# A mixture of experts with soft routing on one core: routing weights read back from DRAM, and weight blocks fetched one by one

## The chip, the core and the metric

The kernel runs on one core of a Trainium2 chip. A core has TensorE for matrix products (PE in the profile; its weight loads stand apart as PEld), VectorE (DVE) and ScalarE (ACT) for elementwise work, GpSimd (POOL), which here mostly issues DMAs, and SyncE (SP), which only issues DMAs. TensorE writes its results to PSUM[...]; everything else on the chip lies in SBUF. The metric is device time in microseconds (us), the median of several runs. A change of under 2% either way counts as "the same".

## The reference

Every one of 8192 rows has 512 values and 8 router logits. The softmax of the logits gives 8 routing weights, and the output row is the sum over the 8 experts of the weight times the row's product with that expert's 512 x 2048 matrix.

```python
batch, seq, hidden, n_experts, expert_hidden = 16, 512, 512, 8, 2048
probs = np.exp(router_logits - logits_max)
probs = probs / np.sum(probs, axis=-1, keepdims=True)
for e in range(n_experts):
    expert_out = np.matmul(x, expert_weights[e])
    output += probs[:, :, e:e+1] * expert_out
```

## The kernel before

The sum over experts is written as one large product: the rows, each scaled by its eight weights and laid side by side, times the stacked expert matrices. That product is cut into 2 x 2 blocks, and a scheme of the Strassen-Winograd kind (seven products of sums and differences in place of eight) is applied to it, in part on two levels. `B11` ... `B22` are the four blocks of the stacked matrices (in the code `11`, `12`, `21`, `22`); each comes as four tiles `w` of 1 MB in float16 (128 x 8 x 512). `z` are the scaled rows, made on VectorE from `xT` (a block of 256 rows, transposed) and `pT` (the routing weights of these rows, the same on all partitions).

The program has a start (rows 0 to 511 at once, without the scheme), four sub-products (numbers 1, 5, 2 and 4), and a main phase, which does the remaining products for all rows. TensorE, VectorE and the other engines each run their instructions in a fixed order; SyncE and GpSimd each issue their DMAs in a fixed order, and an issue that has to wait holds up those behind it.

Two kinds of routing weights are made in the start. A small softmax takes the logits of 512 rows only; a large one takes all rows, and its result goes to DRAM (`p_dram`), from where `load_p` fetches it for a block of 256 rows, the same row to all partitions:

```python
def softmax_of_all():
    pf = softmax(lg_all, J)
    ...
    for r in range(R):                      # four stores
        sp(p_dram[:, :, ds(r * J, J)], ph[ds(r * NHQ, NHQ)])

def load_p(h, first):
    pT = xpool.tile([P, HE, HQ], f16, name="pT", tag="x")
    sp(pT, p_dram[h, ds(first, HE), :].partition_broadcast(P))
    return pT
```

`sp` issues a DMA from SyncE, `pool` one from GpSimd. For rows 512 to 1023 (two blocks of 256) the kernel before does not use `load_p`. It makes diagonal matrices from the small softmax and multiplies a matrix of ones with them, so that TensorE itself spreads the weights over the partitions:

```python
def early_xp1(j, d):
    t, rows = j // 2 - 2, ds(j % 2 * P, P)
    ps = bank()
    for c in range(C):                      # transposes x with an identity
        mm(ps[:, ds(c * P, P)], xs0[:, j, ds(c * P, P)], ident, c == 0, c == C - 1)
    evacuate(xp1[t][0][:, :, rows], ps.rearrange("p (c t) -> p c t", c=C), 0)
    ps = bank()                             # spreads the routing weights
    mm(ps, ones, d.rearrange("p e t -> p (e t)"), True, True)
    evacuate(xp1[t][1][:, :, rows], ps.rearrange("p (e t) -> p e t", e=HE), 1)
```

`evacuate` copies a bank to SBUF, on VectorE for an even last argument and on ScalarE for an odd one. The call stands in the start, among the products for rows 0 to 511:

```python
for n in range(2):
    ps = [bank() for _ in range(4)]
    for e in range(HE):
        ...                                 # 16 matmuls for each n and e
        if n == 1:
            for j in ((4, 5), (6, 7), (), ())[e]:
                early_xp1(j, ds_[j - 4])
            if e == 1:
                sums[0]()
    for j in range(4):
        o = half()
        act(nc.scalar.copy(o, ps[j]))
        sp(kept[1][j // 2][n]..., o)        # results kept in DRAM, 256 KB each
    if n == 0:
        ph0.append(early_p(1))              # the small softmax
        softmax_of_all()
        ds_ = [diag_j(j) for j in range(4, 8)]
        w, sums = inner_sums(b11, new_w())
```

Sub-product 1 follows, with the two blocks as its `xp`. It makes four `z` from them, three sums and a difference of these, and the matching sums `w` of the weight tiles; seven products `prod(p)` of eight matmuls each follow, twice (for `u` = 0 and 1), in the order 1, 2, 5, 6, 3, 7, 4:

```python
a11, a12 = (mul(*xp[0], e0, 2, 0, HQ) for e0 in (0, 2))
a21, a22 = (mul(*xp[1], e0, 2, 0, HQ) for e0 in (0, 2))
s1 = new(a21, a22, ADD)
s2 = new(s1, a11, SUB)
s4 = new(a12, s2, SUB)
tt(a21, a11, a21, SUB)
z = {1: a11, 2: a12, 3: s4, 4: a22, 5: s1, 6: s2, 7: a21}
```

The main phase needs twelve weight tiles at once (`w6`, `w7`, `w3`) out of fifteen that the pool has. `load` has a gate: a tiny memset of the new tile on VectorE, so that the DMA is not issued before VectorE has come to that place. The four tiles of B22 (`w3`) are loaded at the end of sub-product 4, without the gate. In the first pass of the main phase (`q == 0`) they are first used after eight groups of 16 matmuls (four with `w6`, four with `w7`):

```python
def weights_of_main():
    ...
    w3.update({kn: load(22, kn, False) for kn in BLOCKS})
...
for j, tn in enumerate(QUARTERS):           # four groups with w6
    if j > 1:
        rows.load_kept(j)
    x = bank()
    act(nc.scalar.copy(x, rows.m1[tn]))
    ...
    plain(x, 6, w6, tn, False)
    v = half("u")
    tt(v, x, rows.m5[tn], ADD)
```

Of the kernel before, what the change touches and what calls it, by code (L numbers as in the profile page):

```python
# [32 lines left out]
def kernel(  # L33
# [7 lines left out]
    nc = tc.nc  # L41
# [90 lines left out]
    def sp(o, i):  # L132
        note(nc.sync.dma_start(out=o, in_=i))  # L133
# [84 lines left out]
    def cast_x(j):  # L218
        pool(xs0[:, ds(j, 2), :], x_f[ds(j * HQ, HQ), :].rearrange(ROWS[j // 4], p=P))

    def load_lg0(t):
        rows = lg_f.rearrange("(q h) e -> q h e", h=2 * HQ)[ds(2 * t, 2), 0:HQ]
        tile_ = lg0[t].rearrange("p (q j) e -> p q j e", j=2)
        if t == 0:
            sp(tile_, rows.rearrange("q (p j) e -> p q j e", p=P))
        else:
            for q in range(2):
                sp(tile_[:, q], rows[q].rearrange("(j p) e -> p j e", p=P))
    lg0 = [cpool.tile([P, 4, E], f32, name=f"lg0_{t}") for t in range(2)]
    load_lg0(0)  # L230
    cast_x(0)
    cast_x(2)
    ident = cpool.tile([P, P], f16, name="ident")
# [10 lines left out]
    for e in range(2):  # L244
        cast_w(11, BLOCKS[3], e, b11[BLOCKS[3]])

    def early_p(t):
        return softmax(lg0[t], 4, cpool.tile([P, HE, 4], f16, name=f"ph0_{t}"))

    def diag(p):  # L250

        d = h_tile([P, 4, P], f16)
        tt(d, ident.unsqueeze(1).to_broadcast([P, 4, P]), p.to_broadcast([P, 4, P]), MUL)
        return d
# [6 lines left out]


    z0 = [zpool.tile([P, HE, C, P], f16, name="z", tag="z") for j in range(4)]
    ph0 = [early_p(0)]

    def diag_e(e):
        return diag(ph0[0][:, e].unsqueeze(2))

    def early_z0(e, d):
        for j in range(4):  # L270
# [3 lines left out]
            evacuate(z0[j][:, e], ps.rearrange("p (c t) -> p c t", c=C), j)  # L274


    ones = cpool.tile([P, P], f16, name="ones")
    nc.vector.memset(ones, 1.0)
    xp1 = [[xpool.tile([P, C, HQ], f16, name=name, tag="x") for name in ("xT", "pT")] for t in range(2)]

    def diag_j(j):
        return diag(ph0[1][:, :, ds(j % 4, 1)])

    def early_xp1(j, d):
        t, rows = j // 2 - 2, ds(j % 2 * P, P)
        ps = bank()
        for c in range(C):
            mm(ps[:, ds(c * P, P)], xs0[:, j, ds(c * P, P)], ident, c == 0, c == C - 1)
        evacuate(xp1[t][0][:, :, rows], ps.rearrange("p (c t) -> p c t", c=C), 0)
        ps = bank()  # L290
        mm(ps, ones, d.rearrange("p e t -> p (e t)"), True, True)
        evacuate(xp1[t][1][:, :, rows], ps.rearrange("p (e t) -> p e t", e=HE), 1)


    R = 4
# [4 lines left out]

    def load_logits():
        dve(nc.vector.memset(lg_all[:, 0, 0:1], 0.0))
        dve(nc.vector.memset(lg0[1][:, 0, 0:1], 0.0))
        load_lg0(1)
        for r in range(R):
            sp(lg_all[ds(r * NHQ, NHQ)], lg_v[r])

# [134 lines left out]
# [3 lines that stand above are left out]
            if n == 0 and e < 2:  # L445
                early_z0(e + 2, ds_[e + 2])
                if e == 0:
                    ds_.append(diag_e(3))
            for c in range(C):
                for j in range(4):  # L450
                    mm(ps[j], z0[j][:, e, c], b11[e // 2, n][:, e % 2 * C + c, :],
                       e + c == 0, e == HE - 1 and c == C - 1)
            if n == 1:
                for j in ((4, 5), (6, 7), (), ())[e]:
                    early_xp1(j, ds_[j - 4])
                if e == 1:
                    sums[0]()
        for j in range(4):
            o = half()
            act(nc.scalar.copy(o, ps[j]))  # L460
            sp(kept[1][j // 2][n].rearrange("(p j) m -> j p m", j=2)[j % 2], o)
        if n == 0:
            ph0.append(early_p(1))
            softmax_of_all()
            ds_ = [diag_j(j) for j in range(4, 8)]
            w, sums = inner_sums(b11, new_w())

    def weights_of_t1():
# [6 lines left out]
        yield  # L475
        ready[5] = yield from inner_weights(b)
    pinned[0] = False
    x_new.extend((4 + 2 * t, xp1[t][0]) for t in range(2))
    share(xs=3, r=4, o=8)
    sub_product(1, 0, P1, w, weights_of_t1(), 1,  # L480
                xp1, (sums[1], sums[3], sums[2]))
# [36 lines left out]
    def weights_of_main():  # L518
        for kn in BLOCKS:
            t, w7[kn] = load(22, kn), load(12, kn)  # L520
            yield
            tt(w7[kn], t, w7[kn], SUB)
        for kn in BLOCKS:
            w6[kn] = load("t2", kn)
        yield
        w3.update({kn: load(22, kn, False) for kn in BLOCKS})
    share(r=4, o=11)
    sub_product(4, 1, P2, ready[4], weights_of_main())

# [73 lines left out]
        rows.c11(j)  # L603
    pinned[0] = True
    o10 = None
    sums = inner_weights(w3)
    for q in range(NI):
        following = Rows(q + 1) if q + 1 < NI else None

        def ahead(make, k, following=following):  # L610
            if following:
                getattr(following, make)(k)

        def plain(ps, r, w, tn, start):
            t, n = tn
            for k in range(2 * K8):
                mm(ps, rows.z[r][k // K8][:, k % K8, ds(t * P, P)], w[k // K8, n][:, k % K8, :],
                   start, k == 2 * K8 - 1)


        xs, vs = [], []
        for j, tn in enumerate(QUARTERS):
            if j > 1:
                rows.load_kept(j)
            x = bank()
            act(nc.scalar.copy(x, rows.m1[tn]))  # L626
            if o10 and j == 0:
                o10()
            if j > 1 or q == 1:
                rows.c11(j)  # L630
            if j < 2:
                rows.s4(j)
            else:
                ahead("a11", j - 2)
# [3 lines that stand above are left out]
            xs.append(x)  # L638
            vs.append(v)

        banks = {}

        def seeded(b, v, scale=1.0):
            banks[b] = bank()
            act(nc.scalar.mul(banks[b], v, scale))  # L645
        if q:
            seeded("b", vs[0])
            seeded("d", vs[3], -1.0)
            if q == NI - 1:
                seeded("e", vs[3], -1.0)  # L650
        else:
            seeded(0, vs[0])
            seeded(1, vs[1])


        if q == 1:
            inner3 = finish(sums)
        if q:
            z3 = rows.inner()
        for j, tn in enumerate(QUARTERS):  # L660
            x, m5 = xs[j], rows.m5[tn]
            plain(x, 7, w7, tn, False)
            c21 = half("m")
            act(nc.scalar.copy(c21, x))  # L664
            rows.put(1, 0, tn, c21, accum_op=ADD)
            tt(m5, x, m5, ADD)
            rows.put(1, 1, tn, m5)
            if j < 2:
                ahead("s2", j)


        def early(j):
            if following:
                following.load_kept(j)
                if q:
                    following.c11(j)

        ahead("s3", 0)
        if q == 0:
            def c12(j, tn, rows=rows, vs=vs, banks=banks):  # L680
                act(nc.scalar.copy(vs[j], banks[j]))
                rows.put(0, 1, tn, vs[j])

            for j, tn in enumerate(QUARTERS):
                plain(banks[j], 3, w3, tn, False)
                if j < 2:
                    seeded(j + 2, vs[j + 2])
                if j < 3:
                    c12(j, tn)
                if j < 2:  # L690
                    early(j)
                    next(sums)
            ahead("s3", 1)
            o10 = lambda: c12(3, QUARTERS[3])
            rows = following
            continue

        def prod(p, b):
            if b not in banks:
                banks[b] = bank()  # L700
            for k in range(K8):
                mm(banks[b], z3[p][:, k, :], inner3[p][:, k, :],
                   p in (1, 5) and k == 0, k == K8 - 1)
            return banks[b]

        def put(j, *args, rows=rows, vs=vs):
            tt(vs[j], *args)
            rows.put(0, 1, QUARTERS[j], vs[j])

        v00, v01, v11, v10 = vs  # L710
        x = prod(1, "x")
        r1 = half("r")
        act(nc.scalar.copy(r1, x))  # L713
        put(0, prod(2, "b"), r1, ADD)
        early(0)
        r5 = prod(5, "q")
        tt(v11, r5, v11, ADD)
        prod(6, "x")
        tt(v01, x, v01, ADD)
        early(1)  # L720
        put(1, prod(3, "q"), v01, ADD)
        prod(7, "x")
        r3 = half("r")
        act(nc.scalar.copy(r3, x))  # L724
        put(2, x, v11, ADD)
        ahead("s3", 1)
        if q < NI - 1:
            d = prod(4, "d")

            def o10(put=put, r3=r3, d=d):  # L730
                put(3, r3, d, SUB)
        rows = following
# [35 lines left out]
```

## Time and profile before

| What | Before |
|---|---|
| median of 3 runs | 1434.25 us (1433.23 to 1434.26) |
| span of the profiled run | 1434.2 us |
| ScalarE busy | 271.0 us |
| GpSimd busy | 219.6 us |
| moved by DMA | 318.92 MB, 222 GB/s on average |
| longest stretch of TensorE in the chain of waits | 715.03 us, from 48.49 |

In the chain of waits a line is a stretch of the path that ended last: start, length, and what it was. In a timeline a line is a run of like instructions: start, length, engine, line of the kernel, operation, what it writes and reads, how many, and in brackets the idle time before it with what ended it. In the DMA view a line gives a queue or a kind of issue, its number, its size and the median time from issue to landing. A line of the waits names who waited for whom, the total, how often, and the longest.

### The profile page before, as it was taken

Reading aid. Unit: us, or ns where it says so; the run is one execution under the profiler, and the core shown is the slowest. Engines: PE = TensorE matmul, PEld = TensorE weight load, DVE = VectorE, ACT = ScalarE, POOL = GpSimd, SP = SyncE. Lnnn points to the kernel's source line nnn. Section 1 sums busy time; section 2 is a strip of 40 time slices with the busy share of each in tenths; the row PEclk is TensorE's granted clock in tenths of the full one; section 3 lists DMA queues with packets and bytes.
Section 4 is the critical chain, followed back from the end, with each engine's and each line's share of the span. In section 5 each row is a group of like instructions: output and inputs, shape, how many; then the busy total and the mean of one; then the engine's idle time right before and its main releaser. Section 6 shows DMA issues by size and latency. Waiting matters only on the chain.

```text
span 1434.2 us, 18172 instructions
## 1 busy us (share of the span) xinstructions
PE 1424.9 (99%) x6654; PEld 647.9 (45%) x6654; DVE 1032.0 (72%) x1173; ACT 271.0 (19%) x472; POOL 219.6 (15%) x344
## 2 busy tenths in 40 slices
PE   9999999999999999999999999999999999999998
PEld 4444444444444444444444444444444444444444
DVE  6967585656686867766767687777777877877773
ACT  3211111111111111111111211111111111111111
POOL 3111000110001000001000222222222222222220
PEclk9999999999999999999999999999999999999999
DMA  9899967899649994467766967777777767778764
GB/s 196 185 249 266 274 160 191 183 258 259 208 148 301 352 338 147 132 191 222 213 248 206 298 188 238 237 237 233 229 220 226 210 212 214 231 234 242 220 199 103
DMA packets 192041, 318.92 MB, mean 222 GB/s; under 512 B 51664, under 2 KB 80592, under 8 KB 187344
## 3 DMA queue, kind: packets, MB, share of 16 engines
q1 hardware_dynamic: 135328, 202.92, 44.2%
q0 software_dynamic: 56624, 114.84, 34.1%
q8 instruction: 52, 0.85, 0.2%
q14 instruction: 37, 0.30, 0.1%
HBM read 180.13 MB, written 159.58 MB: 237 GB/s over the span
## 4 chain that ended last, share of the span: by engine, by line
PE 93%; issue 3%; DMA 2%; POOL 1%; DVE 0%; ACT 0%; POOLq 0%; SPq 0%; DVEq 0%; ACTq 0%
PE ps L142 93%; POOL out_dram L595 1%; DMA h<-kept 1%; DMA out_dram<-h 1%; DMA w<-in_expert_weights_dram 1%; POOL w L136 0%; DVE z L122 0%; DVE h L122 0%; ACT ps L626 0%; SPq L133 0%; POOLq L595 0%; POOL ident L235 0%; DVEq L122 0%; POOLq L136 0%; POOLq L235 0%
## 5 line engine op out<-in xcount | busy, mean ns | idle before, releaser
L142 PE MATMUL ps<-w,z 128*128 128x512 f16 x6560 | 1415.2, 379 | 3.5 <-ACT ps L626 1.9
L142 PEld LDWEIGHTS <-z 128*128 128x128 f16 x6560 | 641.6, 98 | 776.0 <-issue 2.2
L122 DVE TENSOR_TENSOR h<-ps,h 128x512 f32<-128x512 f32 x389 | 267.7, 689 | 312.9 <-PE ps L142 89.2
L122 DVE TENSOR_TENSOR z<-xT,pT 128x2048 f16<-128x2048 f16 x252 | 304.2, 1218 | 32.5 <-PE ps L142 30.5
L122 DVE TENSOR_TENSOR z<-z 128x2048 f16<-128x2048 f16 x280 | 303.6, 1108 | 7.3
L404 ACT COPY h<-ps 128x512 f32<-128x512 f32 x248 | 145.3, 586 | 602.1 <-PE ps L142 594.9
L595 POOL DMA_DIRECT2D out_dram<-h x244 | 153.7, 663 | 535.4 <-DVE h L122 328.8
L122 DVE TENSOR_TENSOR w<-w 128x4096 f16<-128x4096 f16 x36 | 82.3, 2286 | 0.8 <-DMA w<-wd 0.7
L664 ACT COPY h<-ps 128x512 f32<-128x512 f32 x64 | 37.5, 585 | 177.0 <-PE ps L142 172.4
L136 POOL DMA_DIRECT2D h<-in_x_dram x30 | 21.3, 709 | 263.3 <-DMA xT<-h 226.2
L122 DVE TENSOR_TENSOR h<-h 128x512 f32<-128x512 f32 (+1 forms) x67 | 46.0, 687 | 20.8 <-DMA h<-kept 20.3
L122 DVE TENSOR_TENSOR h<-h,ps 128x512 f32<-128x512 f32 (+1 forms) x78 | 52.7, 675 | 11.0 <-PE ps L142 10.9
L136 POOL DMA_DIRECT2D w<-in_expert_weights_dram x41 | 30.8, 765 | 187.3 <-DVE w L161 131.0
L645 ACT ACTIVATE ps<-h 128x512 f32<-128x512 f32 x35 | 21.0, 602 | 166.9 <-DVE h L122 166.9
L626 ACT COPY ps<-h 128x512 f32<-128x512 f32 x64 | 35.6, 593 | 36.3 <-DMA h<-kept 30.7
L136 POOL DMA_DIRECT2D w<-wd x12 | 6.5, 543 | 189.1 <-DVE w L161 116.1
L724 ACT COPY h<-ps 128x512 f32<-128x512 f32 x15 | 8.8, 585 | 120.7 <-PE ps L142 120.7
L713 ACT COPY h<-ps 128x512 f32<-128x512 f32 x15 | 8.8, 586 | 16.5 <-PE ps L142 16.5
L260 DVE CAST z<-ps 128x512 f16<-128x512 f32 x8 | 5.2, 686 | 4.3 <-PE ps L142 4.3
L136 POOL DMA_DIRECT2D w<-wdt x8 | 4.4, 560 | 21.9 <-DVE w L161 21.9
L260 DVE CAST xT<-ps 128x512 f16<-128x512 f32 x4 | 2.6, 687 | 5.4 <-PE ps L142 5.4
L142 PEld LDWEIGHTS <-w 128*128 128x128 f16 x80 | 5.0, 98 | 2.6 <-DMA w<-in_x_dram 0.9
(37 smaller groups left out, 44.3 us busy)
## 6 DMA issues: line engine op xcount, KB each, us to landing
out_dram<-h POOLq DMA_DIRECT2D x244, 256.0 KB, 4.9
kept<-h SPq DMA_DIRECT2D x192, 256.0 KB, 4.1
h<-kept SPq DMA_DIRECT2D x192, 256.0 KB, 4.6
pT<-p_dram SPq DMA_DIRECT2D x124, 256.0 KB, 5.1
w<-in_expert_weights_dram POOLq DMA_DIRECT2D x39, 512.0 KB, 12.8
out_dram<-h SPq DMA_DIRECT2D x75, 256.0 KB, 3.4
xT<-x SPq DMA_DIRECT2D x62, 256.0 KB, 2.8
w<-wd POOLq DMA_DIRECT2D x12, 1024.0 KB, 10.7
```

Source lines behind the costliest of these rows:

```text
L122: dve(nc.vector.tensor_tensor(out=o, in0=a, in1=b, op=op))
L136: note(nc.gpsimd.dma_start(out=o, in_=i))
L142: nc.tensor.matmul(ps, z, w, start=start, stop=stop, skip_group_check=True)
L260: dve(nc.vector.tensor_copy(o, ps))
L404: nc.scalar.copy(t, ps)
L595: queue.dma_start(out=out_rows(self.q, odd, tn[0], cols, tn[1]), in_=o, **how)
L626: act(nc.scalar.copy(x, rows.m1[tn]))
L645: act(nc.scalar.mul(banks[b], v, scale))
L664: act(nc.scalar.copy(c21, x))
L713: act(nc.scalar.copy(r1, x))
L724: act(nc.scalar.copy(r3, x))
```

## The change

It has two parts. First, the routing weights of rows 512 to 1023 no longer come from a second small softmax, diagonals and products with ones; they are read back from `p_dram` with `load_p`, like those of all later rows. That is meant to take work from TensorE, VectorE and ScalarE in the start. The copies of `xT` now alternate between VectorE and ScalarE. Second, the four tiles of B22 for the main phase are no longer loaded in one go at the end of sub-product 4; they are loaded with the gate between the first groups of the main phase: two at `j` = 1, one at 2, one at 3. That is meant to keep 4 MB of loads away from the moment at which the main phase fetches its first rows and kept results.

```diff
-    def load_lg0(t):
-        ...                                   # logits of 2 x 256 rows, for t = 0 and 1
-    lg0 = [cpool.tile([P, 4, E], f32, name=f"lg0_{t}") for t in range(2)]
-    load_lg0(0)
+    lg0 = cpool.tile([P, 4, E], f32, name="lg0")
+    sp(lg0..., lg_f...)                       # those of t = 0 only
...
-    ones = cpool.tile([P, P], f16, name="ones")
-    nc.vector.memset(ones, 1.0)
-    xp1 = [[xpool.tile([P, C, HQ], f16, name=name, tag="x") for name in ("xT", "pT")] for t in range(2)]
+    x1 = [xpool.tile([P, C, HQ], f16, name="xT", tag="x") for t in range(2)]
-    def early_xp1(j, d):
+    def early_x1(j):
...
-        evacuate(xp1[t][0][:, :, rows], ps.rearrange("p (c t) -> p c t", c=C), 0)
-        ps = bank()
-        mm(ps, ones, d.rearrange("p e t -> p (e t)"), True, True)
-        evacuate(xp1[t][1][:, :, rows], ps.rearrange("p (e t) -> p e t", e=HE), 1)
+        evacuate(x1[t][:, :, rows], ps.rearrange("p (c t) -> p c t", c=C), j)
...
         if n == 0:
-            ph0.append(early_p(1))
             softmax_of_all()
-            ds_ = [diag_j(j) for j in range(4, 8)]
+            xp1 = [(x1[t], load_p(4 + 2 * t, P1)) for t in range(2)]
             w, sums = inner_sums(b11, new_w())
...
-        w3.update({kn: load(22, kn, False) for kn in BLOCKS})
...
             act(nc.scalar.copy(x, rows.m1[tn]))
+            if q == 0 and j:
+                for kn in ((), BLOCKS[:2], BLOCKS[2:3], BLOCKS[3:])[j]:
+                    w3[kn] = load(22, kn)
```

In the fixed order of SyncE the two loads of `pT` stand behind the four stores to `p_dram` and the four stores of the first results to `kept`. In the fixed order of VectorE the products of `xT` and `pT` stand before the sums of the weight tiles.

More of the change, by code (lines that the diff above doesn't have):

```diff
@@ L219, in cast_x @@
         pool(xs0[:, ds(j, 2), :], x_f[ds(j * HQ, HQ), :].rearrange(ROWS[j // 4], p=P))
-    def load_lg0(t):
[L222 to L228, printed above, removed]
-    lg0 = [cpool.tile([P, 4, E], f32, name=f"lg0_{t}") for t in range(2)]
-    load_lg0(0)
+    lg0 = cpool.tile([P, 4, E], f32, name="lg0")
+    sp(lg0.rearrange("p (q j) e -> p q j e", j=2),
+       lg_f.rearrange("(q h) e -> q h e", h=2 * HQ)[0:2, 0:HQ].rearrange("q (p j) e -> p q j e", p=P))
     cast_x(0)
@@ L245 @@
         cast_w(11, BLOCKS[3], e, b11[BLOCKS[3]])
-    def early_p(t):
-        return softmax(lg0[t], 4, cpool.tile([P, HE, 4], f16, name=f"ph0_{t}"))
     def diag(p):
@@ L263 @@
     z0 = [zpool.tile([P, HE, C, P], f16, name="z", tag="z") for j in range(4)]
-    ph0 = [early_p(0)]
+    ph0 = softmax(lg0, 4, cpool.tile([P, HE, 4], f16, name="ph0"))
     def diag_e(e):
-        return diag(ph0[0][:, e].unsqueeze(2))
+        return diag(ph0[:, e].unsqueeze(2))
     def early_z0(e, d):
@@ L274, in early_z0 @@
             evacuate(z0[j][:, e], ps.rearrange("p (c t) -> p c t", c=C), j)
-    ones = cpool.tile([P, P], f16, name="ones")
-    nc.vector.memset(ones, 1.0)
-    xp1 = [[xpool.tile([P, C, HQ], f16, name=name, tag="x") for name in ("xT", "pT")] for t in range(2)]
-    def diag_j(j):
-        return diag(ph0[1][:, :, ds(j % 4, 1)])
-    def early_xp1(j, d):
+    x1 = [xpool.tile([P, C, HQ], f16, name="xT", tag="x") for t in range(2)]
+    def early_x1(j):
         t, rows = j // 2 - 2, ds(j % 2 * P, P)
@@ L302, in load_logits @@
         dve(nc.vector.memset(lg_all[:, 0, 0:1], 0.0))
-        dve(nc.vector.memset(lg0[1][:, 0, 0:1], 0.0))
-        load_lg0(1)
         for r in range(R):
@@ L454 @@
                 for j in ((4, 5), (6, 7), (), ())[e]:
-                    early_xp1(j, ds_[j - 4])
+                    early_x1(j)
                 if e == 1:
@@ L477 @@
     pinned[0] = False
-    x_new.extend((4 + 2 * t, xp1[t][0]) for t in range(2))
+    x_new.extend((4 + 2 * t, x1[t]) for t in range(2))
     share(xs=3, r=4, o=8)
@@ L605 @@
     o10 = None
-    sums = inner_weights(w3)
     for q in range(NI):
@@ L653 @@
             seeded(1, vs[1])
+            sums = inner_weights(w3)
         if q == 1:
```

## The prediction

> **What bounds the kernel now.** I read the page's busy shares first, then the waits of TensorE, then the chain of work that ended last, then the timeline of the first 50 us, and last the DMA view in short windows. The first two say how much there is to win:
>
> ```profile
> PE 1424.9 (99%) x6654; PEld 647.9 (45%) x6654; DVE 1032.0 (72%) x1173; ACT 271.0 (19%) x472; POOL 219.6 (15%) x344
> ```
>
> ```profile
> PE ps L142 <- ACT ps L626: 1.9, 1, 1.9
> PE ps L142 <- DMA w<-in_expert_weights_dram: 1.3, 1, 1.3
> ...
> PE ps L142 <- DVE z L122: 0.3, 1, 0.3
> ```
>
> TensorE is without work for 1434.2 - 1424.9 = 9.3 us, and 1.29 us of that lie before its first instruction. Three waits can be named: 1.3 us at the first weight block, 0.3 us on a VectorE product, 1.9 us on a ScalarE copy. No change that only clears waits can bring 2% (28.7 us). What a new wait can cost has no such bound. The chain shows where the small waits lie:
>
> ```profile
> 10.80 35.64 PE ps L142 x188
> 46.44 0.78 issue
> 47.21 1.23 DVE z L122
> 48.44 0.05 issue
> 48.49 715.03 PE ps L142 x3312
> ...
> 832.68 5.00 DMA out_dram<-h
> ...
> 838.13 5.96 DMA h<-kept
> ...
> 844.17 0.60 ACT ps L626
> ```
>
> Columns: start, length, what. At 46.4 to 48.5 us TensorE is held by a VectorE product; from 48.49 on it runs 715 us without a hole. The VectorE timeline before that point is the base of all that follows (start, length, engine, line, operation):
>
> ```profile
> 29.39 1.29 DVE L260 CAST xT<-ps 128x512 f16<-128x512 f32 x2 [4.83 <-PE ps L142]
> 30.79 2.36 DVE L122 TENSOR_TENSOR z<-xT,pT 128x2048 f16<-128x2048 f16 x2
> 33.73 1.29 DVE L260 CAST xT<-ps 128x512 f16<-128x512 f32 x2 [0.58 <-PE ps L142]
> 34.93 2.28 DVE L122 TENSOR_TENSOR w<-w 128x4096 f16<-128x4096 f16 x1
> 37.13 2.35 DVE L122 TENSOR_TENSOR z<-xT,pT 128x2048 f16<-128x2048 f16 x2
> 39.40 2.28 DVE L122 TENSOR_TENSOR w<-w 128x4096 f16<-128x4096 f16 x1
> 41.60 1.22 DVE L122 TENSOR_TENSOR z<-z 128x2048 f16<-128x2048 f16 x1
> 42.74 2.29 DVE L122 TENSOR_TENSOR w<-w 128x4096 f16<-128x4096 f16 x1
> 44.94 3.49 DVE L122 TENSOR_TENSOR z<-z 128x2048 f16<-128x2048 f16 x3
> ```
>
> From 33.73 us on VectorE never rests, and the last of the three products at 44.94 ends at 48.43, when TensorE starts again at 48.49. So this chain, and not TensorE, sets when the first of the seven-product blocks gets under way, and it has about no slack. It starts with the product of xT and pT at 30.79.
>
> **What the Trainium skill says.** "DMA: Bandwidth & Descriptors", section "Queues, rings and completion order", says that each of the 16 DMA engines alternates between the queues that have work, packet by packet, and takes the descriptors of one queue's ring in their order. The trace agrees: between 28 and 30 us the software queue moves 388 packets and the hardware queue 388. So SyncE's small stores run only one packet for each weight packet, and what SyncE issues later starts behind what it issued before. The same page, "Latency and other measured facts", says that engines 7 and 15 are usually slower; the trace names no engine, but rates fall to a straggler's 23 GB/s after 37 us. "TensorE: Matmul & The Clock Gate", Part 1, says that an idle window of about 3.4 us halves the clock and a busy one restores it. Before, the granted clock is 0.999 of full speed, so no hole in the work has yet done that; I use the page for an estimate below.
>
> **Part 1: the weights of rows 512 to 1023 from DRAM.** Removed: four matmuls with the ones matrix, 0.21 us apart in a dense stretch (64 matmuls from 34.18 take 13.98 us), 0.85 us; four diagonals on VectorE (2.49 us, at 22.07); the small softmax (five short operations from 15.89 to 17.20, 1.3 us); four ScalarE copies into pT; two small loads. Two of the four copies into xT go from VectorE to ScalarE. Added: two loads of pT from p_dram, 256 KB each.
>
> If pT were there in time, the chain would be 1.0 us shorter (the second pair of copies becomes one, 0.6 us, and starts 0.43 us earlier because two ones matmuls are gone), TensorE would come 0.85 us earlier, and some 1 us would be won. So the question is when pT lands. Step by step:
>
> 1. The large softmax starts 1.3 us earlier, at about 15.9, so the four stores to p_dram are issued from about 21.2 instead of 22.47.
> 2. Before, they were slow:
>
> ```profile
> kept<-h SPq DMA_DIRECT2D x4, 256.0 KB, 10.9
> ...
> p_dram<-h SPq DMA_DIRECT2D x4, 48.0 KB, 8.8
> ```
>
> This is from issue to landing, median, over 10 to 40 us. They have 1536 packets of 128 bytes, the first moves about 3.9 us after its issue (none by 26.4), and 194 move per us (388 in 2 us): 8 us. The last landed 10.8 us after an issue at 24.5, at 35.3. Nothing read them before 46 us. Now the packets start 1.3 us earlier into the same saturated engines; the last should land at about 34.0.
> 3. The loads of pT need all four stores: they are issued at about 34.1 and 34.6. In SyncE's order they stand behind the four stores to kept (1 MB), whose packets wait behind those of p_dram.
> 4. Those stores move from about 33 to 36.5 us at near full rate, then one engine goes on alone: from 37.2 to 38.7 the DMA view shows 23 GB/s, and the last store, issued at 28.1, lands at about 39.0. The first pT adds 128 packets of 2 KB, 8 to an engine. At 23 GB/s the slow engine needs 8 x 2 KB / 23 GB/s = 0.7 us more. I put the landing T at 39.7; without the straggler it would be about 37.7.
>
> VectorE runs its instructions in their order, and the two products that read pT stand ahead of everything else in the list. From T: two products 2.28, one copy 0.60, then the unchanged run from 34.93 to 48.43, 13.50. The last product is done at T + 16.4. Before it was at 48.43, so TensorE starts on that block later by T - 32.0: for T = 39.7, 7.7 us.
>
> On the way TensorE does the first two products (16 matmuls, to about 43.8) and then waits for the sum s1, at T + 2.88 + 7.89 = 50.5: idle for 6.7 us. By the skill's page the clock will then be halved: 8 matmuls take 3.4 us instead of 1.7. The next product waits for VectorE until T + 14.1 = 53.8 in any case, so the first 3.4 us are hidden; if the clock is not back by then, up to 1 us more shows. I add 0.3. The 0.85 us of removed matmuls are lost in this wait. Sum of part 1: +8.0 us.
>
> **Part 2: B22's blocks.** Before, GpSimd issued the four 1 MB loads at 781.07, 782.79, 784.52 and 786.25, as product 4 let go of its weights. Now each waits for a small memset on VectorE (0.07 us each) among the first products: by the instruction order two after the first v (795.3), one after the second (about 798 to 800), the last after the third (about 806). A 1 MB load of stored weights takes 10.7 us on the page, so the last is there at about 817. TensorE first reads B22 when its eight groups of 16 matmuls are through: the fourth copy of that stage ends at 819.4, and the late blocks are wanted one group (3.4 us) further on. No wait, therefore. In return the loads of kept issued at 789.50 and 790.73, for which VectorE waited until 799.83, come sooner; TensorE was dense there (680 to 843 us), so that gives nothing. The one wait nearby, 1.9 us at 843 us, hangs on a store at 832.68 and a load behind it at 838.13, well after all this. Sum: 0, perhaps -1 to +1.
>
> **Total.** 1434.25 + 8.0 + 0 = 1442.2 us.
>
> **Rivals.**
> - pT lands by 31 us and the change wins 1 us (1433). For it: fewer matmuls, less VectorE work, a softmax 1.3 us earlier. Against it: stores that took 6.7 to 10.8 us and 1 MB of stores ahead in the queue. It would need a DMA queue that is free at 21 us, and that queue is full to 34. I give it one in twelve.
> - pT lands at about 37.7, as the straggling engine is not the one that matters or is not there: +5.7 us, 1440.
> - The clock stays low for some windows after the pause, or the late start pushes the next loads of x into VectorE's way: 11 to 13 us, 1445 to 1447.
> - The blocks of B22 come late, or the loads of kept collide with them at 795 to 812 and hold a PSUM bank: a few us at 805 to 822. VectorE has about 10 us in hand there, so I hold it unlikely.
> - The clearing of the DMA queues at 781 to 797 also removes the 1.9 us wait at 843: 1440. The chain of that wait starts later, so it is unlikely too.
>
> **Range and chances.** The landing of pT decides: 37.7 to 40.7 gives +5.7 to +8.7, clock and part 2 add -1 to +3. So 1438 to 1446.5 should hold 8 times in 10. Two per cent are 28.7 us either way; TensorE's idle time is only 9.3, and a loss of 28 would need something unseen: faster 0.005, within 2% 0.97, slower 0.025.
>
> **What would show it.** In the profile after: VectorE idle from about 30 to 39.7 us, released by the landing of pT; TensorE idle for some 6 us between 43 and 51 us, and again for shorter times, released by VectorE's z; a granted clock under full there; the long dense stretch from about 56 instead of 48.5 us, and the rest of the program shifted by that much; the wait at about 852 us still there. It is wrong if VectorE does not wait at 30 us, if the stretch starts before 53 or after 60 us, or if new TensorE waits stand near 810 to 830 us.

## The result and the profile after

The changed kernel takes 1443.96 us (median of 6 runs, 1443.51 to 1447.74), the kernel before in the same comparison 1433.59. The ratio is 1.0076 with a 95% interval of 1.0063 to 1.0089: a loss of 0.8%, within the 2% that count as the same, but far outside the scatter. The predicted time was 1442.2, the range 1438 to 1446.5.

The page of the changed kernel, its busy line and its costliest group (busy time and mean of one; after the bar the idle time before, and what ended most of it):

```profile
PE 1426.7 (99%) x6650; PEld 648.3 (45%) x6650; DVE 1027.1 (71%) x1164; ACT 269.6 (19%) x469; POOL 219.6 (15%) x344
...
L142 PE MATMUL ps<-w,z 128*128 128x512 f16 x6560 | 1417.3, 379 | 10.0 <-DVE z L122 8.7
```

VectorE's busy time fell by 4.9 us and ScalarE's by 1.4, TensorE has four matmuls less, and the kernel is slower: TensorE now waits 8.7 us for VectorE's `z`, where it waited 0.3 before. The chain of waits shows where:

```profile
45.88 2.35 DVE z L122 x2
48.23 2.20 DVE w L122
50.43 1.14 DVE z L122
...
51.62 3.55 PE ps L142 x8
...
55.96 1.23 DVE z L122
57.19 0.05 issue
57.23 751.90 PE ps L142 x3483
...
841.42 5.83 DMA out_dram<-h
```

The long stretch of TensorE begins at 57.23 instead of 48.49 us; the store of which the main phase waits is still in the chain. VectorE's timeline tells why the stretch begins late:

```profile
28.70 0.69 DVE L250 CAST xT<-ps 128x512 f16<-128x512 f32 x1 [8.56 <-PE ps L142]
40.80 2.36 DVE L122 TENSOR_TENSOR z<-xT,pT 128x2048 f16<-128x2048 f16 x2 [11.41 <-DMA pT<-p_dram]
43.08 0.68 DVE L250 CAST xT<-ps 128x512 f16<-128x512 f32 x1
43.68 2.28 DVE L122 TENSOR_TENSOR w<-w 128x4096 f16<-128x4096 f16 x1
...
53.69 3.49 DVE L122 TENSOR_TENSOR z<-z 128x2048 f16<-128x2048 f16 x3
```

The bracket of the second line is the whole finding: VectorE stood still for 11.41 us, until pT had landed. All that stands behind is the list of the kernel before, with the same lengths, ten us later at its head and 8.75 us at its end (53.69 instead of 44.94). And SyncE's issues (start of the first, time for the group):

```profile
20.45 2.67 SPq L133 DMA_DIRECT2D p_dram<-h  x4
24.99 1.79 SPq L133 DMA_DIRECT2D kept<-h  x4
33.25 0.82 SPq L133 DMA_DIRECT2D pT<-p_dram  x2
```

The stores to p_dram go out at 20.45; the loads that need them go out at 33.25, and the first is used at 40.80. That makes 12.8 us for the way to DRAM and 7.5 for the way back.

The trace of before with which this is compared came from an execution of 1435.99 us, longer than that kernel's median. So the two spans differ by 8.0 us and the two medians by 10.4.

### The profile page after: what moved, and what is told of

Its sections match the earlier page's. It is cut to its first block, busy times and chain, and to the rows that moved or that the text cites. A ratio compares the mean times of both kernels' runs of the same rounds, so it can differ in the third digit from the quotient of the medians.

```text
span 1442.2 us, 18148 instructions
## 1 busy us (share of the span) xinstructions
PE 1426.7 (99%) x6650; PEld 648.3 (45%) x6650; DVE 1027.1 (71%) x1164; ACT 269.6 (19%) x469; POOL 219.6 (15%) x344
## 4 chain that ended last, share of the span: by engine, by line
PE 93%; issue 2%; DMA 1%; POOL 1%; DVE 1%; ACT 0%; SPq 0%; POOLq 0%; ACTq 0%; DVEq 0%
PE ps L142 93%; POOL out_dram L573 1%; DMA out_dram<-h 0%; DVE z L122 0%; DMA h<-kept 0%; DVE w L122 0%; ACT ps L603 0%; POOL w L136 0%; DVE h L122 0%; SPq L133 0%; POOLq L573 0%; ACTq L603 0%; DVEq L122 0%
## 6 DMA issues: line engine op xcount, KB each, us to landing
w<-in_expert_weights_dram POOLq DMA_DIRECT2D x39, 512.0 KB, 12.8
```

## The experiments

Eight more kernels ran. In the first group of four the kernel before had a median of 1433.95 us, in the second 1434.19; the ratios are to these.

**One part at a time.** The first experiment keeps the routing weights from DRAM and undoes the second part:

```diff
+        w3.update({kn: load(22, kn, False) for kn in BLOCKS})
...
-            if q == 0 and j:
-                for kn in ((), BLOCKS[:2], BLOCKS[2:3], BLOCKS[3:])[j]:
-                    w3[kn] = load(22, kn)
```

> Part 1 alone: routing weights from DRAM, B22's blocks fetched as in the kernel before. Theory A (VectorE waits for pT, which lands near 41 us, and nothing else matters): TensorE runs without a hole from about 57 us as in the changed kernel, time 1443.5 to 1445, that is 10 us above the kernel before. Theory B (a good part of the loss comes from B22's late blocks in the main phase): 1438 or less. Theory C (part 2 gives back some of it): 0.7 us above the changed kernel, the wait near 851 us about 2.3 us instead of 1.6.

Measured: 1444.65 us, ratio 1.0071 (1.0059 to 1.0083). The second does the reverse: the kernel before, with these lines changed the other way.

> Part 2 alone: the kernel before, with B22's four blocks fetched one by one. Theory A: 1432.5 to 1434, no hole on TensorE in the main phase but the one near 843 us, which may shrink by up to 1 us. Theory B: 1437 or more, with new waits of TensorE between 805 and 830 us.

Measured: 1433.76 us, ratio 0.9997 (0.9989 to 1.0005). The waits of TensorE (who for whom, total, times, longest), in the first the routing weights alone:

```profile
PE ps L142 <- DVE z L122: 9.5, 3, 5.9
PE ps L142 <- ACT ps L605: 1.9, 1, 1.9
```

and in the second B22's blocks alone:

```profile
PE ps L142 <- ACT ps L624: 1.0, 1, 1.0
...
PE ps L142 <- DVE z L122: 0.3, 1, 0.3
```

The wait for `z` belongs to part 1, and with it the whole loss. Part 2 makes no measurable difference. It does what it is for: with it GpSimd issues the third of the main phase's early stores at 799.44 us instead of 805.71, as the loads of kept come sooner:

```profile
795.49 1.08 POOL L136 DMA_DIRECT2D w<-wd  x2 [15.07 <-DVE w L161]
798.92 0.53 POOL L136 DMA_DIRECT2D w<-wd  x1 [2.35 <-issue]
799.44 0.55 POOL L594 DMA_DIRECT2D out_dram<-h  x1
802.37 0.53 POOL L136 DMA_DIRECT2D w<-wd  x1 [2.38 <-issue]
```

But TensorE did not wait for these. The wait for ScalarE's copy in the main phase, 1.2 us in the changed kernel, 1.9 before and 1.0 here, looks as if part 2 had shortened it; in the other traces with part 2 it was 1.6 to 2.0, and in the last kernel below, without part 2, 0.3. It scatters by itself, and theory C is not borne out: the median of the weights alone does lie 0.7 us above that of the changed kernel, but its ratio (1.0071) lies below (1.0076).

**Why pT is late.** The third experiment gives the weights of the two blocks a short way: two stores of 2 KB into a DRAM tensor of their own, and the loads ahead of all other stores.

```diff
+        for i in range(2):
+            sp(p_near[i].rearrange("e (r j) -> r e j", r=R), ph[ds(4 + 2 * i, R, NHQ), HE:2 * HE])
+        for i in range(2):
+            sp(near[i], p_near[i].partition_broadcast(P))
+        with behind():                     # the large stores after these on SyncE
             for r in range(R):
                 sp(p_dram[:, :, ds(r * J, J)], ph[ds(r * NHQ, NHQ)])
...
```

> The changed kernel, but the routing weights of the two blocks go first to a small DRAM tensor of their own (32 rows of 128 bytes in two stores) and are read back ahead of the large stores to p_dram and of the stores to kept. Theory A: the place in SyncE's queue and the 1536 small packets make pT late; pT now lands at 29 to 32 us, VectorE waits less than 2 us for it, TensorE is without a hole from about 47 us, time 1431 to 1434, at or a little below the kernel before. Rival D (reading back from DRAM next to the weight loads is slow in itself, whatever the order): pT still lands after 36 us and the time stays above 1439.

Measured: 1434.75 us, ratio 1.0002 (0.9994 to 1.001); the time is 0.75 us above the expected range. One of its 14 executions took 4702 us, for a reason that no trace shows; the ratio leaves it out. SyncE's issues:

```profile
21.31 1.25 SPq L133 DMA_DIRECT2D p_near<-h  x2
26.14 0.97 SPq L133 DMA_DIRECT2D pT<-p_near  x2
27.21 1.34 SPq L133 DMA_DIRECT2D p_dram<-h  x2
28.64 1.99 SPq L133 DMA_DIRECT2D kept<-h  x4
```

and VectorE's timeline:

```profile
31.67 2.36 DVE L122 TENSOR_TENSOR z<-xT,pT 128x2048 f16<-128x2048 f16 x2 [2.25 <-DMA pT<-p_near]
```

From the first store to the issue of the loads 4.8 us pass instead of 12.8, and pT is there 9.1 us earlier. The loss is gone. Rival D falls: reading the weights back is not slow in itself, even beside the weight loads (5.5 us from the issue to the use). The expected gain over the kernel before did not come: VectorE still waited 2.25 us, its chain therefore ended when it had ended before, and TensorE waited 1.3 us for `z` in two pieces.

The next two take the way back apart. The stores to kept behind the loads of pT, nothing else:

```diff
-            sp(kept[1][j // 2][n].rearrange("(p j) m -> j p m", j=2)[j % 2], o)
...
             xp1 = [(x1[t], load_p(4 + 2 * t, P1)) for t in range(2)]
+            with behind():
+                keep_first()               # the same four stores
```

> The changed kernel, with the four stores of first results to kept put behind the two loads of pT in SyncE's order; nothing else. Theory A has two parts: waiting for 1536 small packets, and standing behind 1 MB of kept. Only the second goes: the loads are still issued at about 33.3 us, but land after 5.5 us in place of 7.5, at about 38.8; time about 2 us below the changed kernel, 1441.5 to 1442.5. If the order behind kept were the main thing: pT by 34 us and 1437 or less. If it were nothing: 1443.5 to 1444.5.

Measured: 1441.97 us, ratio 1.0056 (1.0043 to 1.0069). SyncE and VectorE:

```profile
33.57 0.84 SPq L133 DMA_DIRECT2D pT<-p_dram  x2
34.51 2.31 SPq L133 DMA_DIRECT2D kept<-h  x4
```

```profile
37.66 2.36 DVE L122 TENSOR_TENSOR z<-xT,pT 128x2048 f16<-128x2048 f16 x2 [8.02 <-DMA pT<-p_dram]
```

The loads are issued when they were before, as they wait for the small packets, but are used 4.1 us later instead of 7.5. So the place in the queue costs 3.1 us of pT's delay (40.80 - 37.66), one more than expected; the 7.1 us between the issues at 33.25 and 26.14 are the small packets' share. The median is as expected all the same, 2.0 us down and not 3.1. In the trace the start does gain 3.1 us (the last `z` is ready at 54.04 instead of 57.18), but the main phase gives most of it back; the last section says how.

Then the third load of rows (256 KB on GpSimd's queue), held back by two instead of three buffers (`share(xs=2, ...)`):

> The changed kernel, with two instead of three buffers for incoming rows in sub-product 1, so that the third load of rows (256 KB on GpSimd's queue, issued at 23.3 us in the changed kernel, at 39.6 us before) can't run ahead of pT. If that load is what made pT later than predicted (40.8 in place of 39.7): pT about 1 us earlier, time 1442.5 to 1443.3. If it is not: as the changed kernel, 1443.5 to 1444.5.

Measured: 1442.17 us, ratio 1.0054 (1.0041 to 1.0068). The load goes out at 41.15 instead of 23.29, and VectorE has pT at 38.95 instead of 40.80:

```profile
38.95 2.36 DVE L122 TENSOR_TENSOR z<-xT,pT 128x2048 f16<-128x2048 f16 x2 [9.71 <-DMA pT<-p_dram]
```

It is worth 1.8 us, more than expected, and 2.7 us on the way back itself, since the loads of pT went out at 34.12 here. One trace is not exact to a microsecond: in that of the routing weights alone, whose start is the changed kernel's, VectorE had pT at 41.70. The times point the same way: the slowest of this kernel's runs (1442.74 us) is faster than the fastest of the changed kernel (1443.51), though the two ran in different groups and the intervals of their ratios overlap a little.

This load is on another engine's queue and in no line of the diff. GpSimd's issue of it, in the kernel before and then in the changed one:

```profile
39.63 0.71 POOL L136 DMA_DIRECT2D h<-in_x_dram  x1 [17.97 <-DMA kept<-h]
23.29 0.71 POOL L136 DMA_DIRECT2D h<-in_x_dram  x1 [1.83 <-DMA w<-in_expert_weights_dram]
```

In the kernel before it waited for a store to kept to land, whose buffer it took over. In the changed kernel it did not wait for one, ran ahead and shared the DMA engines with the stores to kept. That the buffers are dealt out differently because the diagonals are gone is read from the code; no run tested it.

**Length of the chain, or the clock.** The fourth experiment leaves pT late, but puts the four sums of weight tiles before the products with pT:

```diff
                 if e == 1:
-                    sums[0]()
+                    for i in (0, 1, 3, 2):
+                        sums[i]()          # in this order on VectorE
...
```

> The changed kernel, with the four sums of weight tiles (9 us of VectorE) put before the products of xT and pT in VectorE's order, so that they run while pT is on its way. Theory A: pT lands at 40 to 41 us as before, but the chain behind it is shorter: products from 42 us, the last one at about 50.6, TensorE without a hole from about 50 to 51 us instead of 57.2, time 1437 to 1439. Rival E (the loss comes from the clock that is halved after the pause and from what it does to later stages, not from the length of VectorE's chain): 1441 or more.

Measured: 1440.01 us, ratio 1.0041 (1.0029 to 1.0053), one us above the expected span of times. VectorE's timeline:

```profile
33.49 9.01 DVE L122 TENSOR_TENSOR w<-w 128x4096 f16<-128x4096 f16 x4
42.42 4.62 DVE L122 TENSOR_TENSOR z<-xT,pT 128x2048 f16<-128x2048 f16 x4
...
49.12 0.69 DVE L122 TENSOR_TENSOR h<-ps,h 128x512 f32<-128x512 f32 x1 [0.82 <-PE ps L142]
49.73 3.61 DVE L122 TENSOR_TENSOR z<-z 128x2048 f16<-128x2048 f16 x3
```

The sums now fill the wait, and 4 of the 10 us come back though pT is no earlier. The time lies between the two forecasts; rival E falls in so far as the length of VectorE's chain accounts for these 4 us. Two things in the trace can explain the miss, neither tested by itself. A result's addition (0.69 us) slipped in ahead of the last three `z` and waited 0.82 us for TensorE, which after a pause of 3.7 us ran matmuls at half speed for a while. And the wait in the main phase was 1.8 us, 0.6 longer than in the changed kernel.

**A version that beats both?** Small store, and VectorE's order put right: the first weight sum between the two copies of xT, then all products with pT, the other sums only where TensorE needs them. The same order also in the kernel before.

```diff
                     early_x1(j)
-                if e == 1:
-                    sums[0]()
+                    if j == 4:
+                        sums[0]()
...
+            if rest:
+                rest[0]()
             s1 = new(a21, a22, ADD)
...
-            for make in rest:
+            for make in rest[1:]:
                 make()
```

> The kernel of the small store (routing weights of the two blocks by way of a small DRAM tensor), with VectorE's order changed: the first weight sum between the two copies of xT, the other weight sums behind what TensorE wants first. Theory A (what is left of the loss is the 1.3 us and 0.75 us that TensorE waits for VectorE at 44.5 and 47.4 us): no hole on TensorE from about 15 us to the main phase, time about 2 us below the small store's 1434.75, 1432 to 1433.3, a little below the kernel before. Rival F (run-to-run variation and the wait in the main phase hide it): 1433.7 or more.

> The kernel before, with VectorE's order changed in the same way as in the kernel of small store and order. Theory A: only the hole of 0.71 us at 47.8 us goes, 1433.0 to 1433.5. Together with the first run of this group it says what reading the weights from DRAM is worth when nobody waits for it: the four matmuls with ones, 0.86 us.

Measured: 1433.60 us, ratio 0.9994 (0.9986 to 1.0003), and 1433.21 us, ratio 0.9994 (0.9986 to 1.0002). VectorE in the first:

```profile
29.56 2.28 DVE L122 TENSOR_TENSOR w<-w 128x4096 f16<-128x4096 f16 x1
32.85 0.69 DVE L250 CAST xT<-ps 128x512 f16<-128x512 f32 x1 [1.01 <-PE ps L142]
33.46 4.62 DVE L122 TENSOR_TENSOR z<-xT,pT 128x2048 f16<-128x2048 f16 x4
```

The weight sum fills the wait for pT, and TensorE's waits on `z` are gone from both traces. The waits that remain, of the first

```profile
PE ps L142 <- ACT ps L613: 1.8, 1, 1.8
```

and of the kernel before with the order changed

```profile
PE ps L142 <- ACT ps L628: 0.3, 1, 0.3
```

differ by more than the four matmuls saved (0.86 us at 0.216 us each). Neither version can be told from the kernel before: both intervals hold 1. The mechanism came out as theory A had it, the gain is nearly as small as rival F had it (1433.60 lies between the two forecasts). What reading from DRAM could bring here is below the scatter of one wait in the main phase, 0.3 to 2.0 us in these traces.

## Why the prediction was right

- *The question is when pT lands.* Right. With pT in time by the small store the loss is gone; with part 2 alone there is none.
- *Step 1, the stores 1.3 us earlier, from 21.2.* They were issued from 20.45, 2.0 us earlier: the large softmax began at 15.19, when its logits landed, instead of 17.20.
- *Step 2 and 3, the last store lands at 34.0, the loads go out at 34.1.* They went out at 33.25. The 8 us for the small packets were right, the start was earlier.
- *Step 4, the landing at 39.7.* Used at 40.80. This is the term that was mis-sized: the loads took 7.5 us instead of 5.6. I had the stores to kept moving at near full rate from 33 us on, because the software queue ran dry there before; in the changed kernel it did not, as the third load of rows had been issued 16 us earlier than before (23.29 instead of 39.63). The software queue from 33 to 38 us (packets, MB, share of the engines), before and then in the changed kernel:

```profile
q0 software_dynamic: 199, 0.18, 21.7%
q0 software_dynamic: 448, 0.43, 50.6%
```

  The last store to kept landed at 38.9 us, close to the 39.0 that I had, but not for my reason: I had one slow engine going on alone at 23 GB/s, and from 38 to 39 us the engines still moved 369 GB/s. The first pT then landed 1.8 us behind that store and not 0.7. With the third load of rows held back it landed 0.6 us behind, and pT was used at 38.95. The earlier start and the longer way in part cancelled, which was luck.
- *From T to the restart, T + 16.4.* 40.80 + 16.4 = 57.2; measured 57.23. The chain was counted to 0.1 us, as none of its links changed.
- *TensorE idle for 6.7 us before the third product.* 5.91 us, and 2.39 us before the first, as the first product too had to wait for pT, which the prediction left out. It costs nothing, because the restart hangs on VectorE.
- *The clock halves, up to 1 us.* It did, and cost nothing in the end. The windows of the changed kernel (stretch, its length, busy time and number on TensorE, PEld, VectorE, ScalarE, GpSimd, then the granted clock, the DMA share and GB/s) show it:

```profile
44.00:48.00 4.00, 1.71 (x8) 0.58 (x6) 4.00 (x3) 0.58 (x1) 1.19 (x2) 1.00 0.66 126
48.00:52.00 4.00, 0.38 (x1) 0.13 (x2) 4.00 (x4) 0.00 (x0) 0.07 (x1) 0.52 1.22 269
52.00:56.00 4.00, 4.00 (x13) 1.44 (x12) 4.00 (x4) 0.58 (x1) 0.65 (x1) 0.63 0.94 272
```

  Eight matmuls took 3.55 us in the chain, but VectorE was busy throughout, and its last product, not the slow matmuls, released the restart at 57.19.
- *Part 2: nothing, perhaps -1 to +1.* Right: 0.9997. The last of the four loads came 6.9 us after the first, sooner than the 10.7 us I had counted; TensorE waited for none of them, and the earlier loads of kept gave nothing.
- *The sum.* Predicted +8.0 us, measured +10.4 by the medians. The restart moved by 57.23 - 48.49 = 8.7 us, 0.7 more than the sum had. The wait in the main phase, which scatters, was 0.7 us shorter (1.2 instead of 1.9), so the spans of the two traces differ by 8.0 us; that this is the predicted number is luck. The other 2.4 us lie in the trace of before: it came from an execution 2.4 us longer than the median of 1433.59, and all positions of before were read from it.

## What to carry to other kernels

How long data took to leave for DRAM and come back was set here by the queues, not by the bytes. Ask how many packets stand ahead at that moment, in this queue and in those that share its engines. Taking work off VectorE and ScalarE, which had time for it, gained nothing here, while a new wait at the head of an in-order list delayed all that stood behind it; so before taking work out, look at what the first consumer will wait for, and put independent work in front of it. A change that takes fewer buffers can let a transfer on another queue start sooner, into the way of the one that matters.

## What the runs showed of the hardware

Small packets suffered beside large ones: 1536 packets of 128 bytes (196 KB) took about 8 us, one for each 1 KB packet on GpSimd's queue (388 of each from 28 to 30 us in the kernel before), so these stores moved at some 25 GB/s while the engines moved over 200. With 32 such packets in place of 1536 the loads behind them could be issued after 4.8 us in place of 12.8.

Whether a pause halved the clock did not depend on its length alone. In the trace with kept behind, TensorE paused once more in the main phase, waiting 2.0 us for a ScalarE copy. That is shorter than the window of about 3.4 us with which the prediction reckoned, and yet it then ran 12 matmuls in 4 us instead of 20:

```profile
844.00:848.00 4.00, 4.00 (x20) 1.83 (x19) 3.84 (x5) 0.00 (x0) 0.54 (x1) 1.00 0.74 249
848.00:852.00 4.00, 1.95 (x10) 0.78 (x8) 2.52 (x3) 1.12 (x2) 0.54 (x1) 0.98 0.42 159
852.00:856.00 4.00, 4.00 (x12) 1.47 (x11) 0.00 (x0) 0.00 (x0) 0.00 (x0) 0.59 0.63 188
```

The 2720 matmuls from there to the end took 587.22 us, against 585.53 in the changed kernel. Together with the longer wait (2.05 us against 1.18) that is where most of the gain of the start went.

In other traces waits of 1.9 us there did nothing of the kind, and in that of the routing weights alone even 3.2 us at the start did not: the next 16 matmuls ran at full speed.

```profile
42.98 3.63 PE L142 MATMUL ps<-w,z 128*128 128x512 f16 x16 [3.23 <-DVE z L122]
```

What decides it is not shown. The times of the kernel with kept behind fall in two groups, 1441.2 to 1442.0 and 1443.1 to 1443.5 us, and the profiled execution was the longest; that the clock makes the two groups was not tested.
